# Other rates for the column sums of w_ada and w_in between the weight units

## The chip, the cores and the metric

The kernel runs on one core of a Trainium2 chip. The metric is the time of one execution in microseconds (us) as the device measures it; the lower the better. The core has five engines with queues of their own: TensorE (PE in the profile, its weight loads PEld), VectorE (DVE), ScalarE (ACT), GpSimd (POOL) and SyncE (SP), which issues most of the loads.

## The reference, cut to what matters

One layer of a hybrid decoder, for 512 tokens of width 2048, in float32:

```python
mod = silu(c) @ w_ada + b_ada                       # six rows of 2048
sh_a, sc_a, gt_a, sh_f, sc_f, gt_f = split(mod, 6)
h = rmsnorm(x, norm_mix) * (1 + sc_a) + sh_a
p = h @ w_in                                        # q, k, v, z, c_q, c_kv, k_pe, b, a, gates
y_a = mla(c_q, c_kv, k_pe, ...) @ w_o_mla           # latent attention
y_b = gated_delta_net(q, k, v, z, b, a) @ w_o_gdn   # GDN
g_a, g_b = split(sigmoid(gate_logits), 2)
x = x + gt_a * ((g_a * y_a + g_b * y_b) @ w_o)
h = rmsnorm(x, norm_ffn) * (1 + sc_f) + sh_f
gate, up = split(h @ w_gate_up, 2)
out = rmsnorm(x + gt_f * ((silu(gate) * up) @ w_down), final_norm)
```

`c` is one vector. Each of the six rows of `mod` is therefore 2048 sums of products of one vector with a column of `w_ada`. They are computed on VectorE beside the large products of TensorE, and so is the product of `sh_a` with the columns of `w_in` that belong to the gate `g_a`, which gives that gate a bias.

## The kernel before

**Weight units.** TensorE multiplies in float32r: each operand is split into a rounded part (hi) and the rest (lo), and each product is three matmuls, hi x hi, hi x lo and lo x hi. The work is cut into units. A weight unit loads two 128x512 blocks of a weight (512 KB, SyncE's queue), splits them (ScalarE casts hi at L270, VectorE subtracts lo at L271, both 128x1024) and runs 24 matmuls with 512 columns. kb's units have 12. `Unit` has a `load`, a `split`, and the matmuls `mms`; any of them may be missing.

**The driver** (L51 to L129) takes units from one list. `fill` keeps two units with matmuls ready (`deep`) and four more units of any kind loaded (`ahead`); it calls `load` and `split` in the list's order. `run` emits a unit's matmuls. After each 12 matmuls (`GROUP`) it calls `pump`, which advances each of the side chains by one step: the convolution, the GDN's recursion, the norms of the latents (steps with `cT`, L991 and L250), attention. Those steps have small matmuls of TensorE and operations of VectorE and ScalarE that read their results from PSUM. PSUM has eight banks; a set of weight units holds four of them, and the chains' steps share the rest. The orders on TensorE, SyncE and GpSimd are held as they are written; on VectorE and ScalarE that is so where the code says it, as for the column sums (`late=True`, L443).

**The list** is `mixed(mixing(), extras(), plan)`, L132. `mixing` gives the weight units of the mixer in this order, with the index i that `mixed` counts over all of its units:

- i = 0 loads two small vectors; 1 to 16 the units of the gate logits g_a that the head left over (ga8, ga12)
- 17 to 24 q03, 25 to 32 k03, 33 to 40 v03 (q, k, v of the GDN's heads 0 to 3), 41 to 44 kb (the narrow columns), 45 to 60 gb0 and gb1 (gate logits g_b)
- 61 to 84 q47, k47, v47; 85 to 116 z0, cq, ckv, z1; 117 to 122 qpe, v0, v1; 123 to 130 qk
- 131 to 146 gb2: eight weight units, and ahead of each a unit that only reloads two blocks of the activation h (four tiles of 256 KB) that had been stored to make room; 147 to 154 gb3
- from 155 on ya, yb and w_o; then the channel mixer, whose units do not count (`alone`) or come after the extras are used up

The GDN of heads 0 to 3 runs as a chain from gb0 on, that of heads 4 to 7 from z0 on, attention from qk to the start of ya.

**The extras** (L566) are units without matmuls that `mixed` puts between the weight units. 128 of them are column sums of w_ada, four chunks of 32: a load of 128x1024 (512 KB) and one VectorE operation (`mod_sum`, L442) that multiplies by silu(c) and adds up along the row. The first chunk is the mixer's shift sh_a, without which h isn't complete, then come the channel mixer's scale and shift and the gate gt_a. Number 129 stores gt_a (GpSimd's queue). Numbers 130 to 161 are the column sums of w_in: a load of 512 KB and two VectorE operations (`ada_units`, L384); after each eight of them a chain step brings the sum into columns with four one-column matmuls (`adac`). Behind them the generator gives empty units until attention has ended, then the last chunk of w_ada and the last gate's weights.

**The rate.** `plan(i)` says how many extras follow on the unit with index i. `mixed` adds it up to n and gives one extra for each whole number; a unit marked `alone` adds nothing, but counts in i.

Of the kernel before, what the change touches and what calls it, by code (L numbers as in the profile page):

```python
# [173 lines left out]
def block_kernel(ctx: ExitStack, tc: tile.TileContext, a: dict, out):  # L174
# [17 lines left out]
    def S(s, dt=F32):  # L192
        return slots.tile([P, 512], dt, tag="s", name=nm(s))
# [7 lines left out]
    def load(dst, src):  # L201
        nc.sync.dma_start(dst, src)
# [368 lines left out]
    def head():  # L571
# [39 lines left out]
        for k in range(KT):  # L611
            if k + 1 < KT:
                prepare(k + 1)
            else:
                drv.deep = 1
                drv.open(mixed(everything(), extras(), plan))
            u, head_units[k] = head_units[k], None
            u.pre()
            for m in u.mms:
                m()  # L620
            u.post()
# [617 lines left out]
    def gate_done(n):  # L1239
        def done(ps):  # L1240
            for j in range(4):
                s = S("sg")
                nc.scalar.activation(s[:], ps[j][:], AF.Sigmoid)
                nc.scalar.dma_start(gb_dram[4 * n + j], s[:])
        return done
# [361 lines left out]
    known = set()  # L1607

    def plan(i):
        return 2.0 if i < 16 else 0.7 if i < 48 else 1.0 if i < 150 else 1.2  # L1610

    def act(fn):
        return Unit(load=fn)
# [32 lines left out]
    def reload(k0):  # L1646
        for k in (k0, k0 + 1):
            hN[k] = [S("hh", F32R), S("hl", F32R)]
            for j in range(2):
                load(hN[k][j][:].bitcast(F32), hspill[k, j])  # L1650
# [3 lines left out]
    def w_in_fm(name, c0, done, lo_eng=None):  # L1654
        return fm_set(name, lambda k0, nk: plain(w_in, k0, nk, c0, 512), 512, KT, hx, done, lo_eng=lo_eng)
# [4 lines left out]
    def mixing():  # L1660
# [51 lines left out]
        for n in (2, 3):  # L1712
            us = w_in_fm(f"gb{n}", O_GB + 512 * n, gate_done(n))
            for i, u in enumerate(us):
                if n == 2:
                    yield act(lambda i=i: reload(2 * i))
                yield u
        yv = lambda k: (yT[k][0][:], yT[k][1][:])
        w_om, w_og = a["w_o_mla"][0], a["w_o_gdn"][0]
# [844 lines left out]
    def everything():  # L2564
        yield from mixing()
        yield from ffn()
# [56 lines left out]
```

## Time and profile before

| | |
|---|---|
| median of 3 runs | 2712.14 us (2709.2 to 2715.04) |
| profiled execution, own time | 2706.44 us |
| its span, first to last instruction | 2704.6 us |
| DVE busy | 2087.6 us, 77% of the span |
| ACT busy | 1201.6 us, 44% |
| moved by DMA | 600.45 MB, mean 222 GB/s |
| DVE: sums of w_ada (L442), 192 with the head's 32 and the last chunk's 32 | 233.9 us |
| DVE: sums of w_in (L384), 60 | 44.8 us |
| DVE: lo of the weights (L271), 262 | 320.7 us |

The profile is one execution. Its times run from the first instruction of the program. A row of the busy times by stage has the stretch (from:to), its length, then for each engine the busy time and the number of instructions, the granted clock of TensorE (1.00 is full), the mean busy share of the 16 DMA engines and the rate. A row of waits has who waited, the line of what it waited for and its tile, the sum in us, the number of waits and the longest. A row of a group of instructions has line, engine, operation, what it writes and reads, its shapes, the count, the busy sum in us, the mean of one in ns, and the idle time ahead of it. A row of the timeline has the start, the duration, the instruction, and in brackets the idle time ahead of it with what ended it. All matmuls stand at line 157.

### The profile page before, as it was taken

What the parts mean: (1) busy time and instruction counts of PE and PEld (TensorE: products, weight loads), DVE (VectorE), ACT (ScalarE), POOL (GpSimd) and SP (SyncE); (2) the same over time, 40 slices, a digit from 0 to 9 for tenths busy, and PEclk for the clock granted to TensorE, in tenths of its full rate; (3) what the DMA queues carried; (4) which work ended last, traced back from release to release, by engine and by line L of the source; (5) the groups of instructions that cost most, each with busy time, mean ns of one, the idle gap of its engine ahead of it and who ended that gap; (6) DMA issues with size and microseconds to landing.
All of it is one profiled execution on the core that took longest, in us unless ns stands there. A gap on an engine that the chain in (4) does not pass through costs nothing.

```text
span 2704.6 us, 36528 instructions
## 1 busy us (share of the span) xinstructions
PE 2683.6 (99%) x13046; PEld 2237.3 (83%) x13046; DVE 2087.6 (77%) x3230; ACT 1201.6 (44%) x1720; POOL 228.6 (8%) x310
## 2 busy tenths in 40 slices
PE   9999999999999999999999999999999999999998
PEld 7888788888888888888888888888888888888886
DVE  8785666777768866768788778788878888788786
ACT  3443432453245333234574444444444446545454
POOL 0000002011100000000010000001101101011012
PEclk9999999999999999999999999999999999999999
DMA  9897565646664867854763566567767777788595
GB/s 372 306 351 268 158 192 177 201 152 191 187 172 136 286 223 285 306 187 134 272 193 120 193 209 208 202 218 250 243 227 263 252 249 212 210 238 226 179 278 154
DMA packets 312126, 600.45 MB, mean 222 GB/s; under 512 B 42852, under 2 KB 69636, under 8 KB 311816
## 3 DMA queue, kind: packets, MB, share of 16 engines
q1 hardware_dynamic: 257160, 486.52, 54.7%
q0 software_dynamic: 21888, 59.83, 8.3%
q10 hardware_dynamic: 32896, 51.78, 5.2%
q8 instruction: 102, 1.67, 0.3%
q14 instruction: 80, 0.66, 0.1%
HBM read 507.80 MB, written 90.20 MB: 221 GB/s over the span
## 4 chain that ended last, share of the span: by engine, by line
PE 98%; DVE 1%; ACT 1%; issue 0%; DMA 0%; SPq 0%; DVEq 0%; ACTq 0%
PE m L157 43%; PE gb L157 6%; PE v L157 4%; PE z L157 3%; PE ya L157 3%; PE ga L157 3%; PE k L157 3%; PE s L157 3%; PE q L157 3%; PE yb L157 3%; PE wo L157 3%; PE gu L157 3%; PE dn L157 2%; PE qk L157 2%; PE dnt L157 2%; PE ckv L157 2%
## 5 line engine op out<-in xcount | busy, mean ns | idle before, releaser
L1888 ACT CAST hi<-raws 128x1024 fp32r<-128x1024 f32 (+1 forms) x360 | 322.9, 907 | 575.3 <-DVE raws L1868 346.9
L1895 DVE TENSOR_TENSOR lo<-raws,hi 128x1024 fp32r<-128x1024 f32 (+1 forms) x360 | 376.0, 1046 | 176.5 <-ACT hi L1888 168.9
L270 ACT CAST hi<-raw 128x1024 fp32r<-128x1024 f32 x262 | 271.9, 1041 | 489.8 <-DMA raw<-in_w_in_dram 130.7
L271 DVE TENSOR_TENSOR lo<-raw,hi 128x1024 fp32r<-128x1024 f32 x262 | 320.7, 1227 | 190.2 <-ACT hi L270 183.6
L442 DVE CUSTOM_DVE_ANT_0 rawm<-rawm,cbc 128x1024 f32<-128x1024 f32 x192 | 233.9, 1234 | 3.8 <-DMA rawm<-in_w_mod_dram 3.5
L157 PE MATMUL m<-hi,h2h 128*128 128x512 f32 x480 | 190.7, 397 | 0.0
L157 PE MATMUL m<-hi,h2l 128*128 128x512 f32 x480 | 187.4, 390 | 0.0
L157 PE MATMUL m<-lo,h2h 128*128 128x512 f32 x480 | 186.9, 389 | 0.0
L157 PE MATMUL m<-hi,xh 128*128 128x512 f32 x448 | 174.6, 390 | 0.7 <-DVE al L247 0.7
L157 PE MATMUL m<-hi,xl 128*128 128x512 f32 x448 | 174.4, 389 | 0.0
L157 PE MATMUL m<-lo,xh 128*128 128x512 f32 x448 | 174.4, 389 | 0.0
L1895 DVE TENSOR_TENSOR lo<-sums,hi 128x1024 fp32r<-128x1024 f32 x120 | 146.7, 1222 | 22.2 <-ACT hi L1888 22.1
L1868 DVE TENSOR_TENSOR sums<-raws,raws 128x1024 f32<-128x1024 f32 x120 | 146.2, 1219 | 3.6 <-DMA raws<-in_w_down_dram 3.6
L1888 ACT CAST hi<-sums 128x1024 fp32r<-128x1024 f32 x120 | 126.1, 1051 | 36.1 <-PE m L157 22.5
L157 PEld LDWEIGHTS m<-hi,h2l 128*128 128x128 f32 x480 | 90.1, 188 | 19.4
L157 PEld LDWEIGHTS m<-lo,h2h 128*128 128x128 f32 x480 | 90.4, 188 | 17.8
L157 PEld LDWEIGHTS m<-hi,h2h 128*128 128x128 f32 x480 | 90.2, 188 | 17.3
L157 PE MATMUL gb<-hh,hi 128*128 128x512 f32 x256 | 102.4, 400 | 0.0
L157 PE MATMUL gb<-hh,lo 128*128 128x512 f32 x256 | 100.0, 391 | 0.0
L157 PE MATMUL gb<-hl,hi 128*128 128x512 f32 x256 | 99.9, 390 | 0.0
L157 PEld LDWEIGHTS m<-hi,xh 128*128 128x128 f32 x448 | 84.1, 188 | 18.8 <-DVE al L247 1.1
L157 PEld LDWEIGHTS m<-hi,xl 128*128 128x128 f32 x448 | 84.1, 188 | 17.6
(587 smaller groups left out, 6844.5 us busy)
## 6 DMA issues: line engine op xcount, KB each, us to landing
raws<-in_w_gate_up_dram SPq DMA_DIRECT2D x400, 256.0 KB, 4.0
rawm<-in_w_mod_dram SPq DMA_DIRECT2D x192, 512.0 KB, 5.5
raw<-in_w_in_dram SPq DMA_DIRECT2D x144, 512.0 KB, 5.0
raws<-in_w_down_dram SPq DMA_DIRECT2D x160, 256.0 KB, 5.2
s_dram<-raws ACTq DMA_DIRECT2D x88, 256.0 KB, 3.5
raws<-s_dram SPq DMA_DIRECT2D x88, 256.0 KB, 4.3
rawa<-in_w_in_dram SPq DMA_DIRECT2D x32, 512.0 KB, 5.6
raw<-in_w_o_dram SPq DMA_DIRECT2D x24, 512.0 KB, 6.9
```

Source lines behind the costliest of these rows:

```text
L157: return self.tc.keep_in_program_order(f(*args, **kwargs))
L270: nc.scalar.copy(hi[:], raw[:])
L271: (lo_eng or nc.vector).tensor_tensor(lo[:], raw[:], hi[:].bitcast(F32), ALU.subtract)
L442: r = nc.vector.tensor_tensor_reduce(raw, raw, c, 1.0, 0.0, ALU.mult, ALU.add, parts[:, k, half:half + 1])
L1868: add = lambda o, x, y: behind(nc.vector.tensor_tensor(o, x, y, ALU.add))
L1888: nc.scalar.copy(hi[:], src)
L1895: nc.vector.tensor_tensor(lo[:], src, hi[:].bitcast(F32), ALU.subtract)
```

## The change

Two edits. `plan` gets other rates: 0.6 instead of 0.7 for i from 16 to 25, 1.2 instead of 0.7 or 1.0 from 26 to 59, 0.9 instead of 1.0 from 60 to 115; from 116 on, and below 16, it is as before. And the eight units of gb2 that reload activations are marked `alone`, so that they add nothing to n.

```diff
     def plan(i):
-        return 2.0 if i < 16 else 0.7 if i < 48 else 1.0 if i < 150 else 1.2
+        return 2.0 if i < 16 else 0.6 if i < 26 else 1.2 if i < 60 else 0.9 if i < 116 else 1.0 if i < 150 else 1.2
...
                 if n == 2:
-                    yield act(lambda i=i: reload(2 * i))
+                    yield Unit(load=lambda i=i: reload(2 * i), alone=True)
                 yield u
```

`act(fn)` is `Unit(load=fn)`, so `alone` is the only difference in the second edit.

## The prediction

> **What bounds the kernel now.** I read the page first, then the waits of TensorE, then the busy time by stage of the stretch that the change touches.
>
> ```profile
> span 2704.6 us, 36528 instructions
> PE 2683.6 (99%) x13046; PEld 2237.3 (83%) x13046; DVE 2087.6 (77%) x3230; ACT 1201.6 (44%) x1720; POOL 228.6 (8%) x310
> PEclk9999999999999999999999999999999999999999
> ```
>
> TensorE is busy for 2683.6 of 2704.6 us at the full granted clock; 21.0 us are idle in all. The stages, in the order of the rows below: the two last ga sets, q03, k03 with v03, kb, gb0 with gb1, q47 to v47, z0 to z1, qpe to qk, gb2 with gb3, ya with yb; the last row is the kernel's end.
>
> ```profile
> core 0: us, PE busy (x) PEld busy (x) DVE busy (x) ACT busy (x) POOL busy (x), PEclk, DMA share, GB/s
> 100.00:188.00 88.00, 88.00 (x391) 72.57 (x391) 78.08 (x133) 34.75 (x48) 3.88 (x8) 1.00 0.95 336
> 188.00:232.00 44.00, 44.00 (x195) 36.45 (x195) 30.60 (x40) 18.84 (x25) 2.13 (x4) 1.00 1.00 370
> 232.00:319.00 87.00, 87.00 (x385) 72.07 (x384) 49.13 (x70) 32.62 (x44) 0.00 (x0) 1.00 0.55 171
> 319.00:330.00 11.00, 11.00 (x50) 7.11 (x49) 9.21 (x15) 5.77 (x10) 0.00 (x0) 1.00 0.34 106
> 330.00:431.00 101.00, 101.00 (x500) 84.40 (x498) 65.91 (x125) 34.30 (x44) 16.79 (x11) 1.00 0.60 184
> 431.00:576.00 145.00, 145.00 (x895) 120.93 (x894) 103.39 (x198) 57.72 (x89) 10.79 (x18) 1.00 0.60 188
> 576.00:788.00 212.00, 209.15 (x1244) 175.40 (x1243) 165.58 (x365) 84.49 (x141) 28.85 (x31) 1.00 0.60 181
> 788.00:903.00 115.00, 115.00 (x665) 100.16 (x664) 87.92 (x213) 53.59 (x117) 1.17 (x1) 1.00 0.55 164
> 903.00:1032.00 129.00, 127.72 (x694) 110.09 (x694) 86.90 (x197) 48.30 (x93) 0.00 (x0) 1.00 0.67 229
> 1032.00:1210.00 178.00, 178.00 (x802) 147.36 (x802) 124.71 (x184) 55.19 (x68) 6.60 (x11) 1.00 0.82 285
> 2650.00:2700.00 50.00, 44.26 (x196) 36.32 (x194) 36.30 (x91) 19.64 (x45) 18.42 (x15) 0.99 0.60 149
> ```
>
> Only two of the ten stages have an idle TensorE: 2.85 us in z0 to z1 and 1.28 us in gb2 with gb3, 4.13 us together. That is the whole of what moving sums about between 100 and 1210 us can take out of idle time; the rest lies in the head and the tail, which the change leaves alone. The waits of TensorE between 100 and 1210 us say who ends these idle times, and the rows of one stage ahead say what the weights wait for.
>
> ```profile
> engine line waited for: us in total, times, longest us
> PE cT L157 <- DVE cql L250: 1.6, 1, 1.6
> PE cq L157 <- ACT sz L946: 0.9, 1, 0.9
> PE adac L157 <- DVE yl L247: 0.6, 1, 0.6
> PE sc L157 <- DVE knl L247: 0.5, 1, 0.5
> PE cq L157 <- ACT E L766: 0.3, 1, 0.3
> ...
> ACT hi L270 <- PE gb L157: 47.1, 13, 6.2
> ACT hi L270 <- PE k L157: 23.7, 7, 4.4
> ACT hi L270 <- DMA raw<-in_w_in_dram: 18.0, 8, 6.9
> ```
>
> No wait of TensorE is for a weight (hi or lo of a matmul of this stretch). It is the other way round: in q03 to gb1 the casts of ScalarE (L270) wait for TensorE to give a buffer back. How far ahead they are, DVE's splits and the chain of waits show:
>
> ```profile
> 309.47 1.23 DVE L271 TENSOR_TENSOR lo<-raw,hi 128x1024 fp32r<-128x1024 f32 x1 [4.05 <-ACT hi L270]
> ...
> 319.46 11.04 PE kb L157 x48
> 330.50 8.16 PE gb L157 x36
> ```
>
> This split, counted in the order of the units, is that of gb0's first unit; it ends at 310.70 and its matmuls start at 330.50. The weights are 19.8 us ahead.
>
> **What the change does, counted by hand.** I add up the rate over the unit index i and note each whole number. Numbers 1 to 32 are column sums of w_ada for the mixer's shift, 33 to 128 those of three more chunks, 129 only stores gt_mix, 130 to 161 are the sums of w_in, and after them come empty units until attention ends. Sums that fall in each stage, before and after: ga 32 and 32 (rate 2.0 up to i = 15 is untouched); q03 6 and 5; k03 with v03 11 and 18; kb 3 and 8; gb0 with gb1 15 and 19; q47 to v47 24 and 22; z0 to z1 32 and 29; qpe to qk 14 and 14; gb2 16 and 8; gb3 to i = 154 9 and 9. Nothing is added or removed: 153 and 152 are done when gb2 ends, number 161 falls at i = 153 or 154, and the empty units take up the difference. So from ya on the order is the old one to about a unit. No matmul is added either; each of the four bias sets still makes its few one-column products.
>
> What a sum costs DVE is in these groups:
>
> ```profile
> L442 DVE CUSTOM_DVE_ANT_0 rawm<-rawm,cbc 128x1024 f32<-128x1024 f32 x192 | 233.9, 1234 | 3.8 <-DMA rawm<-in_w_mod_dram 3.5
> L442 DVE DVE_READ_ACCUMULATOR2_ANT parts<- 128x1 f32 x192 | 16.0, 84 | 0.0
> L384 DVE SCALAR_TENSOR_TENSOR acc<-rawa,sh_mix,acc 128x512 f32<-128x512 f32 x60 | 44.8, 747 | 1.2 <-DMA rawa<-in_w_in_dram 0.5
> ```
>
> A w_ada sum is 1.23 + 0.08 = 1.32 us of DVE, a w_in sum two of 0.747, 1.49 us.
>
> *More in the middle.* k03 to kb get 12 more (14 to 26): 15.8 us of DVE. DVE is busy for 49.13 + 9.21 = 58.3 of 98 us there, so it comes to 74 of 98. gb0 with gb1 get 4 more: 65.91 + 5.3 = 71 of 101. Both lie below the 78.08 of 88 that the ga stage carries with TensorE never idle. Were it all laid end to end it would still be less than the 19.8 us by which the weights lead. Each sum loads 128 x 1024 x 4 bytes, 0.52 MB; 12 of them in 98 us add 64 GB/s to the 171 and 106 of these rows, where q03 moved 370. So the cost is 0 by this reckoning. The bounds: not below 0, since no idle time is there to win; above, every added sum could hold up a small chain step, which I price as a rival. I take 0, the nearest row (ga, at rate 2.0 and without idle time) being on that side.
>
> *Fewer behind the head, q47 to z1.* TensorE waits for nothing in q03, so one sum less gains 0. In z0 to z1 the largest wait is cT for cql, and its neighbours on DVE are
>
> ```profile
> 767.37 0.74 DVE L250 SCALAR_TENSOR_TENSOR ckvl<-cT,columns,ckvh 128x512 fp32r<-128x512 f32 x1
> 768.03 1.22 DVE L442 CUSTOM_DVE_ANT_0 rawm<-rawm,cbc 128x1024 f32<-128x1024 f32 x1
> 769.17 0.09 DVE L442 DVE_READ_ACCUMULATOR2_ANT parts<- 128x1 f32 x1
> 769.17 1.22 DVE L442 CUSTOM_DVE_ANT_0 rawm<-rawm,cbc 128x1024 f32<-128x1024 f32 x1
> 770.31 0.09 DVE L442 DVE_READ_ACCUMULATOR2_ANT parts<- 128x1 f32 x1
> 770.31 0.41 DVE L855 TENSOR_SCALAR T64T<-X 32x256 f32<-32x256 f32 x1
> 770.65 0.73 DVE L250 SCALAR_TENSOR_TENSOR cql<-cT,columns,cqh 128x512 fp32r<-128x512 f32 x1
> ...
> 771.44 0.66 PE L157 MATMUL cT<-kc,ckv 128*128 128x128 f32 x4 [1.56 <-DVE cql L250]
> ```
>
> Two sums stand ahead of cql. Counted in their order they are numbers 122 and 123, of z1's last two units. After the change numbers 129 and 130 stand there: a store without DVE work, and a w_in sum. So 2 x 1.22 becomes 1.49 us: 0.9 us less queue, and the wait falls by 0.9 (bounds 0, if cql waits for its matmul or cast instead, and 1.56, all of it). The two waits of cq are for Exp and Silu on ScalarE, with no sum in front: 0. The store itself goes one stage forward; its issue is on GpSimd, busy for 28.85 of 212 us there, and what could come to stand behind it there (the memsets of the GDN's triangular blocks) would wait only for gt_mix, which DVE makes right ahead: 0.
>
> *Reloads not counted.* gb2 gets 8 sums instead of 16: 12 us of DVE and 4.2 MB of loads less. The idle time in this row is the wait of adac for yl (0.6) and of sc for knl (0.5), both on DVE operations that the w_in sums precede. adac also moves by some units, so that its step can meet another step of attention. Bounds: 0 to 1.1 gained; I take 0.4, as adac's wait can come back elsewhere.
>
> **Sum.** -0.9 - 0.4 = -1.3 us. Against the profiled execution (2706.44 us, of which 2704.6 are the span) that is 2705.1; the median of the runs shown is 2712.14, 5.7 above it, and the same -1.3 gives 2710.8.
>
> **A rule that speaks for more.** The steady pace of TensorE in this trace is a matmul each 227 ns:
>
> ```profile
> 232.42 43.52 PE k L157 x192
> L157 PEld LDWEIGHTS m<-hi,h2l 128*128 128x128 f32 x480 | 90.1, 188 | 19.4
> ```
>
> 43.52 / 192 = 0.2267 us, and one weight load takes 0.188, so a stretch without any wait shows 0.188 / 0.2267 = 83% of weight loading. The rows agree: k03 with v03, with no idle time, has 72.07 / 87 = 83%, the same as z0 to z1 (175.40 / 212 = 83%) and the whole span. The Trainium skill, "Trainium Kernel Development and Optimization", section "Performance Expectations", says that busy time of the matmuls is a bad measure of the distance from the limit, and the share of weight loading a good one. By that rule 17% of the span could be open, and a better order of the sums could win more than the 4.13 us. By these rows it isn't: 83% is what an uninterrupted stream gives here.
>
> **Rivals.** (1) *All idle time of the stretch goes.* For it: three of the five waits are on DVE. Against: the two of cq are not. It gives 2712.14 - 4.1 = 2708.0. (2) *Hidden slack of the pipeline*: matmuls that the page counts as busy start late behind small steps, and less DVE work shortens that. It would have to be over 1.3 us on top of (1), 2706.7 or less. Against it: the equal 83% above. (3) *Slower: DVE's queue in gb0 and gb1.* There the GDN's first half begins, one step for 12 matmuls (2.7 us), and each step's PSUM read is on DVE. If the added sums stand in front of these reads as the two did in front of cql, each such place costs up to 1.56 us. It decides from the point where DVE runs more than a step, 2.7 us, behind; four places make 6.2 us, 2718.4. For it: 19 sums instead of 15, and DVE at 71 of 101 us. Against: 32 sums in z0 to z1, with DVE at 165.58 of 212, made one such place. (4) *No effect*: the empty units absorb the count, cql is held by the new sum as long as by the old ones, and the median stays at 2712.1.
>
> **How the numbers follow.** My forecast has a chance of 0.70, (1) 0.12, (2) 0.03, (3) 0.07, (4) 0.08. A measurement can tell about 0.2%, 5.4 us. Only (2) passes it on the fast side, and (1) where scatter of the runs adds 1.3 us, half of its chance: with a little for what I overlook, 0.11. On the slow side (3) and a little: 0.09. The rest, 0.80, is the same. The range: the lowest run shown is the profiled one, 2706.44; less both DVE terms at their ends (1.56 + 1.1) that is 2703.8. The highest is 2715.04, and one new place of 1.56 us makes 2716.6.
>
> **What would show it.** Right: cT's wait for cql under 1 us; the cq waits as they are; DVE at about 74 us in k03 to kb and about 12 us less in gb2, where the DMA rate falls too; TensorE without a wait between 188 and 576 us. Wrong: new waits of TensorE for DVE in gb0 and gb1, or for a hi or lo; a wait of over 2 us anywhere in the stretch; or a matmul pace in k03 other than 227 ns.

## The result and the profile after

| | before | after |
|---|---|---|
| median of 22 runs each, side by side | 2711.26 us | 2713.51 us |
| ratio, 95% interval | | 1.0013 [1.0007, 1.0019] |
| profiled execution | 2706.44 us | 2713.24 us |
| its span | 2704.6 us | 2711.4 us |

The change makes the kernel slower by 0.13%, 3.5 us (1.9 to 5.2). The ratio goes by the fast runs alone, without one of before at 2982.46 us, and so isn't the quotient of the two medians, which lie 2.3 us apart. The loss is less than the 0.2% named in the prediction and inside its range, but the interval does not contain 1, and the forecast pointed the other way: -1.3 us. The two profiled executions lie 6.8 us apart; the one of before is among the fastest of its kernel.

The page's lines on the span and the engines, after:

```profile
span 2711.4 us, 36526 instructions
PE 2687.3 (99%) x13046; PEld 2240.2 (83%) x13046; DVE 2084.2 (77%) x3230; ACT 1200.9 (44%) x1720; POOL 234.3 (9%) x310
```

TensorE does the same 13046 matmuls. Its waits between 100 and 1210 us, after, in the columns of the prediction's view:

```profile
PE X L157 <- issue: 3.9, 5, 1.1
PE gb L157 <- DVE yl L247: 1.2, 2, 0.6
PE cq L157 <- ACT sz L946: 0.9, 1, 0.9
PE sc L157 <- DVE knl L247: 0.5, 1, 0.5
PE cq L157 <- ACT E L766: 0.3, 1, 0.3
```

The wait of cT for cql is gone, as forecast. The largest is new: 3.9 us in X, the 32x32 products of the GDN's second half, for which the profile shows no releaser ("issue"). By stage, after, k03 with v03, kb, gb0 with gb1, and z0 to z1 (columns as in the prediction):

```profile
232.00:319.00 87.00, 87.00 (x386) 72.06 (x385) 56.49 (x87) 30.34 (x42) 0.00 (x0) 1.00 0.64 208
319.00:330.00 11.00, 11.00 (x49) 7.17 (x48) 9.39 (x14) 7.10 (x12) 0.00 (x0) 1.00 0.37 108
330.00:431.00 101.00, 101.00 (x497) 84.28 (x496) 70.78 (x137) 35.01 (x45) 16.81 (x11) 1.00 0.69 214
576.00:788.00 212.00, 206.76 (x1199) 172.84 (x1198) 156.04 (x349) 81.80 (x139) 30.01 (x32) 0.98 0.55 163
```

Of these rows only z0 to z1 (576 to 788) lost anything: TensorE is idle for 5.24 us instead of 2.85, and the granted clock is 0.98. (gb2 with gb3, 903 to 1032, went from 1.28 us of idle time to 1.69.) The order of events there, on TensorE, first before (start, duration, instruction):

```profile
769.10 0.19 PE L157 MATMUL X<-T32T,M 32*32 32x32 f32 x1
...
771.44 0.66 PE L157 MATMUL cT<-kc,ckv 128*128 128x128 f32 x4 [1.56 <-DVE cql L250]
771.85 0.48 PE L157 MATMUL z<-hi,hh 128*128 128x512 f32 x1
...
773.99 0.39 PE L157 MATMUL z<-hi,hh 128*128 128x512 f32 x1
```

and after:

```profile
769.18 0.19 PE L157 MATMUL X<-M,T32T 32*32 32x32 f32 x1
770.13 0.22 PE L157 MATMUL X<-T32T,M 32*32 32x32 f32 x2 [0.76 <-issue]
...
774.47 0.21 PE L157 MATMUL X<-T32T,M 32*32 32x32 f32 x1 [0.96 <-issue]
...
774.80 0.24 PE L157 MATMUL X<-T32T,M 32*32 32x32 f32 x1
...
775.87 1.06 PE L157 MATMUL cT<-kc,ckv 128*128 128x128 f32 x4
776.58 0.78 PE L157 MATMUL z<-hi,hh 128*128 128x512 f32 x1
...
780.53 0.39 PE L157 MATMUL z<-hi,hh 128*128 128x512 f32 x1
```

Read the starts. The last X is 5.70 us later than before (774.80 against 769.10); the first z only 4.73 (776.58 against 771.85), since cT no longer waits 1.56, though its own matmuls are slower (1.11 and 1.06 us instead of 0.66); its tenth matmul 6.54 (780.53 against 773.99), because nine z matmuls take 3.95 us instead of 2.14, some 427 ns apart: TensorE runs at half clock. The granted clock reads 0.50 from 773.6 to 780.5 us, so it fell already between the last stops. From there the difference moves between 6.1 and 8.3 us, as waits of about 1 us come and go in attention and gb2, and ends at 6.9: +0.4 by these, and 0.45 had been there from the head on.

What stands beside it is the store of gt_mix. GpSimd's row of it, before:

```profile
804.89 1.17 POOL L157 DMA_DIRECT2D m_dram<-gt_mix  x1 [40.05 <-DVE gt_mix L449]
```

and after:

```profile
763.36 1.17 POOL L157 DMA_DIRECT2D m_dram<-gt_mix  x1 [19.43 <-DVE gt_mix L449]
```

It writes 128x16 values of 4 bytes, each to an address of its own: 2048 pieces, 8 KB. (The pieces are counted from the address pattern in the code; the DMA view lists this store as 48 packets.) The DMA view of 763 to 776 us has the rate in 40 slices of 0.325 us, and each issue's size and median time to landing. Before:

```profile
GB/s 202 252 254 254 378 266 235 96 203 271 252 290 240 169 109 113 214 214 302 328 265 101 44 154 206 310 317 304 213 151 210 184 301 328 302 202 50 0 0 0
raw<-in_w_ukv_dram SPq DMA_DIRECT2D x4, 256.0 KB, 4.0
```

and after:

```profile
GB/s 326 304 265 186 180 230 323 284 257 174 93 29 8 0 0 0 0 0 0 0 0 2 6 17 46 19 6 5 6 25 14 5 11 3 14 14 27 27 71 217
raw<-in_w_ukv_dram SPq DMA_DIRECT2D x2, 256.0 KB, 10.6
```

From 766.9 us on hardly anything moves for 8 us, and two weight blocks that are asked for at its start, at 767.2 and 767.6 us, take 10.6 us in the median instead of 4.0. The X burst (64 products, 128 matmuls and 128 weight loads) falls into this gap. The trace of before had shown the price of the store in its own place; the same view there, 803 to 822 us, slices of 0.475 us:

```profile
GB/s 0 86 121 345 405 192 129 216 255 274 204 49 1 0 0 0 4 39 69 52 34 60 22 39 22 22 39 26 22 134 328 392 267 136 142 309 318 217 46 22
m_dram<-gt_mix POOLq DMA_DIRECT2D x1, 8.0 KB, 10.5
```

8 KB take 10.5 us to land, and the rate falls to between 0 and 70 GB/s for about 8 us, in a stretch (788 to 903 us) in which TensorE never waits.

### The profile page after: what moved, and what is told of

Its sections match the earlier page's. It is cut to its first block, busy times and chain, and to the rows that moved or that the text cites. A ratio compares the mean times of both kernels' runs of the same rounds, so it can differ in the third digit from the quotient of the medians.

```text
span 2711.4 us, 36526 instructions
## 1 busy us (share of the span) xinstructions
PE 2687.3 (99%) x13046; PEld 2240.2 (83%) x13046; DVE 2084.2 (77%) x3230; ACT 1200.9 (44%) x1720; POOL 234.3 (9%) x310
## 4 chain that ended last, share of the span: by engine, by line
PE 98%; DVE 1%; ACT 1%; DMA 0%; issue 0%; SPq 0%; DVEq 0%; ACTq 0%
PE m L157 43%; PE gb L157 6%; PE v L157 4%; PE z L157 3%; PE ya L157 3%; PE k L157 3%; PE ga L157 3%; PE q L157 3%; PE s L157 3%; PE yb L157 3%; PE wo L157 3%; PE gu L157 3%; PE dn L157 2%; PE dnt L157 2%; PE ckv L157 2%; PE cq L157 2%
```

## The experiments

Theory A: the store's 2048 small pieces hold up the other DMA traffic, and a dense burst on TensorE that meets this gap stops, and the clock falls with it. Its rival B: the sums moved on DVE are the cost, and X only stands where it shows.

**One edit alone, and the store itself.** Four kernels beside the kernel before (33 runs, median 2709.57 us). The first has the new rates only (its edit against the changed kernel):

```diff
-                    yield Unit(load=lambda i=i: reload(2 * i), alone=True)
+                    yield act(lambda i=i: reload(2 * i))
```

> Only the new rates; the reloads of gb2 count as before. Theory A (the store of gt_mix into m_dram in 4-byte pieces keeps the DMA engines from moving anything else for about 10 us; the new rates put it at 763 us, right ahead of the GDN's burst of 32x32 matmuls at 768, whose instructions then don't arrive): number 129 stays at z1's last but one unit, so the waits of the X matmuls for issue (3.9 us) and the slow matmuls behind them are there, and the time is that of the changed kernel, 1.0010 to 1.0015 of before. Rival B (the sums that no longer follow the reloads in gb2 are what costs): as before, 0.9995 to 1.0005. Rival C (the added sums in k03 to gb1 hold up VectorE): as A in time, but with waits of TensorE for DVE between 232 and 441 us.

2713.2 us, 1.0013 [1.0004, 1.0022]: all of the loss, with the store at 763.18 us and TensorE's wait

```profile
PE X L157 <- issue: 4.1, 4, 2.2
```

The second has `alone` only (the old `plan`):

> Only the second edit, with the old rates. Theory A: number 129 falls at v1 as before, its store is issued near 805 us, the X matmuls at 768 run without a wait: within 0.05% of before, or up to 1 us faster by the waits of gb2. Rival B: slower by the 3 us of the changed kernel, 1.0013. Rival C: as before.

2711.93 us, 1.0007 [0.9999, 1.0016]; the store stays late, at 807.56 us, and X does not wait. The time is not told apart from before. The profiled execution isn't free of waits, though: cT waits for ckvl (2.2 us, two times) and cql (1.6), and gb once for yl, behind which half clock follows, as TensorE's rows show:

```profile
909.57 0.65 PE L157 MATMUL gb<-hh,hi 128*128 128x512 f32 x1 [2.42 <-DVE yl L247]
910.02 0.63 PE L157 MATMUL gb<-hl,hi 128*128 128x512 f32 x1
910.44 0.63 PE L157 MATMUL gb<-hh,lo 128*128 128x512 f32 x1
```

The third is the changed kernel with the store moved behind the sums of w_in, and an empty unit in its place:

```diff
-        yield Unit(split=lambda: side(m_dram.rearrange("(k p) -> p k", p=P), gt_mix[:]))
-        known.add(4)
+        yield Unit()
...
+        yield Unit(split=lambda: side(m_dram.rearrange("(k p) -> p k", p=P), gt_mix[:]))
+        known.add(4)
```

> The changed kernel with an empty unit in place of number 129, and the store of gt_mix behind the four sums of w_in (number 162, in ya). Theory A: no wait for issue at 770 us, the matmuls behind the burst run at 227 ns; 5 to 6 us less than the changed kernel, 2707 to 2709, which is also below before by 2 to 4 us. Rivals B and C: the loss stays, 1.0010 to 1.0015 of before.

2707.14 us, 0.9992 [0.9983, 1.0000], no wait in X. The store did not go where I meant it to: GpSimd had nothing else to do, so it was issued only a few instructions later, behind the memsets of TT, which wait for TensorE. Its row, and TensorE's stretch (columns as in the prediction's rows by stage):

```profile
770.52 1.18 POOL L157 DMA_DIRECT2D m_dram<-gt_mix  x1 [0.30 <-issue]
```

```profile
770.00:775.00 5.00, 5.00 (x150) 4.39 (x150) 2.78 (x6) 2.53 (x6) 1.40 (x2) 1.00 0.53 107
775.00:780.00 5.00, 5.00 (x28) 4.18 (x27) 3.85 (x6) 4.87 (x11) 0.00 (x0) 1.00 0.00 0
```

Seven microseconds are enough: the burst (the row with 150 matmuls) is through before the gap, and then 5 us without any traffic cost TensorE nothing. (Part of that silence is that nothing was asked for: SyncE issued no load between 769.7 and 777.7 us.) The fourth leaves the store in place and writes rows of 64 bytes, 128 pieces instead of 2048. The gate then comes back in another order, so this kernel serves for its time alone:

```diff
-        yield Unit(split=lambda: side(m_dram.rearrange("(k p) -> p k", p=P), gt_mix[:]))
+        yield Unit(split=lambda: side(m_dram.rearrange("(p k) -> p k", p=P), gt_mix[:]))
```

> The changed kernel with the same store at the same place, but written in 64-byte rows instead of 4-byte pieces (the gate gt_mix of w_o comes back permuted, so the output is another). Theory A, if the pieces are the cause: as e3, 5 to 6 us below the changed kernel, with the DMA rate from 766 to 776 us near 200 GB/s instead of under 20. If any store at that place does it: the loss stays. Rivals B and C: the loss stays.

2707.07 us, 0.9989 [0.9980, 0.9998], no wait in X. The same queue and 8 KB, issued at 763.52, land in 3.5 us instead of 10.5, and the two weight blocks asked for at 767.4 and 767.9 us in 3.2 instead of 10.6 (DMA view, 763 to 776 us):

```profile
raw<-in_w_ukv_dram SPq DMA_DIRECT2D x2, 256.0 KB, 3.2
m_dram<-gt_mix POOLq DMA_DIRECT2D x1, 8.0 KB, 3.5
```

So it is neither the queue nor the bytes, but into how many pieces they are cut.

**The suspect added to the kernel before.** A copy of 128x16 values, stored in the same 4-byte pieces to a tensor that nobody reads, with the place of the sums unchanged (beside the kernel before: 30 runs, 2709.65 us, for these four):

```diff
+            if n == 24:
+                def again(split=u.split):
+                    split()
+                    behind(nc.vector.tensor_copy(twin[:], parts[:, :, 0]))
+                    side(d_dram.rearrange("(k p) -> p k", p=P), twin[:])
+                u.split = again
...
```

> The kernel before, with a second store in 4-byte pieces: behind sum number 121 a copy of a 128x16 tile goes to a tensor that nobody reads, so that it is issued near 764 us, where the changed kernel has its store. Nothing else of the order changes. Theory A (a store in 4-byte pieces just ahead of the 32x32 burst takes the instructions of TensorE away): waits of the X matmuls for issue of 3 to 5 us and slow matmuls behind them; 4 to 6 us slower than before, 1.0015 to 1.0022. Rival D (the rates do it in another way and the store is only a sign): as before, 0.9997 to 1.0003.

2716.07 us, 1.0023 [1.0013, 1.0033]. The second store, at 763.12 us, brings the whole picture into the kernel before:

```profile
PE X L157 <- issue: 3.6, 3, 1.7
PE cT L157 <- DVE cql L250: 1.6, 1, 1.6
```

with 62 and 20 GB/s between 765 and 775 us. No sum was moved, and the loss is there: rival B isn't needed for it. The counterpart, the kernel before with its only store later (the third kernel's edit):

> The kernel before with an empty unit as number 129 and the store behind the w_in sums (number 162, in ya), as in the run of the changed kernel with a late store. It tells what the rates are worth without the store: if the step of the prediction on cql and adac is right, this is 1 to 2 us slower than the changed kernel with the late store (2707.1). Theory A: the place at 805 us costs the kernel before something in part of its runs (its runs spread from 2706.6 to 2715.3), so 1 to 2 us below before. If the place at 805 us is free: as before.

2709.59 us, 1.0000 [0.9991, 1.0009]. It tells little: the store left at 805.15 us, where it had been. GpSimd has nothing else to issue between the two places in the list, so in both kernels the store goes as soon as gt_mix is there.

**The other half of the condition.** The changed kernel with the store as it is, and the X burst of the second half three steps sooner:

```diff
-        yield 6
+        yield 3 if g else 6
...
-        yield
+        yield 4 if g else 1
```

> The changed kernel, where the second GDN half's burst of 32x32 matmuls (X) comes three steps, 8 us, sooner, near 760 us, and the next step waits three steps longer, so the rest stays. The store in 4-byte pieces stays near 764 to 768 us. Theory A with the burst as the second condition: no wait of X for issue, 4 to 6 us below the changed kernel, though the DMA rate has its gap of 8 to 10 us as there. If the store alone costs the time (weights or loads late): the loss stays at 1.0010 to 1.0015 of before.

2706.40 us, 0.9987 [0.9978, 0.9995], the lowest median here; its interval overlaps those of the third and the fourth kernel. The store takes as long as ever, and the rate shows the same gap, though in part because SyncE asks for nothing between 763.5 and 771.5 us here (DMA view, 763 to 776 us):

```profile
GB/s 148 279 254 199 82 195 208 321 328 177 147 74 46 3 2 0 0 0 0 0 0 0 0 0 0 0 0 0 0 0 0 0 0 0 0 8 14 65 173 340
m_dram<-gt_mix POOLq DMA_DIRECT2D x1, 8.0 KB, 10.5
```

but the burst ran at 758 us, and TensorE has matmuls of 512 and 128 columns in it:

```profile
765.00:770.00 5.00, 5.00 (x31) 4.27 (x30) 1.54 (x3) 4.89 (x11) 0.41 (x1) 1.00 0.40 83
770.00:775.00 5.00, 5.00 (x27) 4.16 (x26) 4.01 (x6) 3.58 (x6) 0.00 (x0) 1.00 0.07 1
```

The loss needs both, store and burst, at one time; either alone costs nothing that these runs show. Next, the changed kernel with the store in four parts of 512 pieces, each behind the eight sums that it belongs to:

```diff
+        def gate_done4(ks):
+            mod_columns(gt_mix, ks, b_cols[:, GT_A // P:GT_A // P + 16])
+            side(m_dram.rearrange("(k p) -> p k", p=P)[:, ks], gt_mix[:, ks])
...
+        yield Unit()
```

> The changed kernel with the store of gt_mix in four parts of 512 pieces, each issued when its four columns are ready (sums 104, 112, 120 and 128), and an empty unit as number 129. Theory A: each part takes a quarter of the 10 us, 2 to 3 us of a low DMA rate; the last, at 763 us, is over when the burst needs its instructions, so no wait for issue or under 1 us of it; 4 to 6 us below the changed kernel, 2707 to 2709. If the number of pieces doesn't set the length: loss as in the changed kernel.

2711.3 us, 1.0007 [0.9998, 1.0016]: a miss. The last quarter, at 765.26 us, still stops X:

```profile
PE X L157 <- issue: 1.3, 2, 1.1
```

A quarter of the pieces leaves a third of the wait, and the time is not told apart from that of before. The control for the sooner burst is the same edit in the kernel before (15 runs, 2710.52 us):

> The kernel before with its own rates, and only the burst of 32x32 matmuls (X) of the GDN's second half three steps sooner, the wait behind it three steps longer, as in the fastest kernel so far. Theory A (the store beside the burst is what costs; the place of the burst by itself is worth nothing): in the kernel before the store lies 40 us behind the burst, so nothing is there to win: the time of the kernel before within 1 us, ratio 0.9996 to 1.0004, no wait in X in either place, and the 2.5 to 3 us that the kernel with the changed rates and the sooner burst is faster than before belong to the rates. Rival (the sooner burst is itself what is worth those 2.5 to 3 us, because small steps of the GDN come free sooner): 2706 to 2707, ratio 0.9987 to 0.9992, and the idle time of TensorE between 760 and 790 us falls.

2709.8 us, 0.9999 [0.9990, 1.0008]. X does not wait in it. The burst's place by itself is worth nothing that can be measured; where the store doesn't disturb it, there is nothing to win.

**What X waits for.** TensorE's instructions seem to be loaded in blocks: one instruction queue shows 102 packets of 16 KB, and 13046 matmuls with as many weight loads make about 256 instructions for each. In the profiles the first stop fell near a block's end. So two kernels put more instructions ahead of the burst, by doing small products of an earlier step twice or more, which moves the blocks' ends within the burst (the first of them; cut to the lines that matter):

```diff
+                    for _ in range(2 if g and c < 3 else 1):
+                        mm(p1[pb:pb + 32, n0:n0 + 32], LT[c][pa:pa + 32, 128 * i + pb:128 * i + pb + 32],
+                           T32[pa:pa + 32, n0:n0 + 32], start=True, stop=True, tile_position=(pa, pb))
```

and the other with `2 + c % 2 if g else 1`.

> The changed kernel with 24 of the 32 small products into M1 (the step six steps ahead of the X burst, second half of the GDN) done twice with the same operands: 24 products of two matmuls and two weight loads each are 96 more instructions of TensorE's stream ahead of the burst, about 0.4 us of work; store and burst stay where they were. In the four profiles with the wait, X first stops about 183 to 193 records behind the start of the burst, and that is 252 to 273 records behind the fetch of a block of TensorE's instructions before it (blocks of 256). Theory A1 (it is the instruction stream that runs dry beside the store: the stop stands at a block's end): the first stop comes about 96 records sooner, 85 to 100 records behind the start of the burst; the wait is 3 to 5 us in all, the time 2712 to 2716 us. Rival A2 (something that each instruction writes or takes runs full, a count from the burst's start): the first stop stays at 183 to 193 records of the burst.

> The changed kernel with the 32 small products into M1 done two or three times: 48 products more, 192 instructions of TensorE's stream ahead of the burst, about 0.8 us of work; store and burst stay where they were. Theory A1 (instruction stream): the end of the block falls within 10 records of the start of the burst and the next one at its end, so the burst either stops near its start (up to record 10) or, if the fetch of the next block has time enough, not at all or only at its last records. Rival A2 (a count from the burst's start): the first stop stays at 183 to 193 records of the burst with the same 4 us.

1.0008 [0.9997, 1.0019] and 1.0012 [1.0001, 1.0024], with 2.1 and 4.4 us of waits in X. TensorE's rows with a stop in X, with 96 more:

```profile
771.95 0.50 PE L157 MATMUL X<-T32T,M 32*32 32x32 f32 x2 [1.82 <-issue]
773.58 0.50 PE L157 MATMUL X<-T32T,M 32*32 32x32 f32 x2 [0.26 <-issue]
```

and with 192 more:

```profile
771.43 0.18 PE L157 MATMUL X<-T32T,M 32*32 32x32 f32 x1 [1.33 <-issue]
774.70 0.25 PE L157 MATMUL X<-T32T,M 32*32 32x32 f32 x1 [3.08 <-issue]
```

Counted in the trace, matmuls and weight loads, the first stop stands 197 and 189 instructions behind the start of the burst; in the four earlier profiles with the wait it was 183 to 193. It did not move by 96 or 192: the end of a block is not what stops X. The five stops in the changed kernel agree, for they lie within 25 instructions, and a block's end could make one of them. The Trainium skill, "Runtime: NRT & Kernel Launch", section "Instruction fetch mechanics", says that crossing such a block costs little and is mostly hidden; in these two runs no stop goes with a block's end. What remains is a count: some 190 instructions of the burst pass within 1.0 to 1.2 us, and then TensorE stops. That something fills up which only the DMA's traffic can empty would fit, but no run here shows it. Nor is it settled where the count starts: from the issue of the store to the first stop it is 230 to 246 matmuls and weight loads, about as constant. Every run here, the timed ones too, comes with its span and granted clock, so all seem to have been recorded; whether an execution without a record would stop as well is not known.

## Why the prediction was wrong

**The step that failed** is the one on the store: "The store itself goes one stage forward; its issue is on GpSimd [...] what could come to stand behind it there [...]: 0." It asked what stands behind the store on its issuing engine, and not what stands behind it in the DMA engines. Its price was 3.9 us of stops and 1.8 us by half clock in the nine z matmuls behind them, in the profiled execution. The runs: adding such a store costs 1.0023; taking it out of the burst's way, by later issue, larger pieces or a sooner burst, gives 0.9992, 0.9989, 0.9987. The place could have been seen, too: the units were counted far enough to put number 129 into z1's last units, where X runs, and the landing time of 10.5 us for 8 KB stood in the trace of before.

**Two sums ahead of cql, -0.9.** Right, and more than forecast: the wait vanished, 1.56, the bound that was named. It isn't the stop of X that gave DVE the time, for the wait is gone too in the kernels without a stop (late store, 64-byte rows, sooner burst). The forecast left a w_in sum of 1.49 us ahead of cql; with 64-byte rows DVE shows no sum at all between 763 and 775 us. In the changed kernel the gain was given back in the same 10 us.

**gb2, -0.4.** Not seen; it came out as +0.4, outside the bounds of 0 to 1.1 gained. adac's wait for yl went, but gb now waits for yl (1.2 us, two times): a step of attention meets a DVE queue at another unit, as feared. The sizes were off as well: in 903 to 967 us DVE is busy for 44.64 us instead of 49.42, 4.8 less and not 12, as the next rows show (before, then after):

```profile
903.00:967.00 64.00, 63.34 (x358) 55.05 (x358) 49.42 (x122) 23.30 (x50) 0.00 (x0) 1.00 0.81 285
```

```profile
903.00:967.00 64.00, 62.93 (x353) 54.60 (x352) 44.64 (x112) 23.16 (x50) 0.00 (x0) 1.00 0.78 264
```

**More sums in the middle, 0.** Right: no wait of TensorE between 188 and 576 us. In k03 to kb DVE came to 56.49 + 9.39 = 65.9 us, not 74. Part of that is a slip in the count: kb has four units, which at a rate of 1.2 give 5 sums and not 8, so that 9 more were due, 11.9 us. The trace has 8 more (22 instead of 14 operations on rawm between 232 and 330 us) and DVE 7.5 us more. In gb0 with gb1 it came to 70.78, the forecast's 71. The cost of 0 doesn't hang on the slip.

**The rivals.** (3), DVE's queue in gb0 and gb1, did not occur; the slow side came by a mechanism that none of them named. (4) is refuted by cql's wait. (1) did not occur as described: both waits of cq are still there. (2) was not tested. Without the meeting of store and burst the changed kernel runs at 0.9987 to 0.9992 of before, 2.2 to 3.5 us less; the forecast ratio for -1.3 us, 0.9995, lies at the edge of these intervals or within them, so the sum of its terms may have been right in size, or somewhat small; by time alone (1)'s -4.1 us would fit as well. Where more than cql's 1.6 us came from was not settled, but one pattern points to it: in all five profiles with the old rates cT waits for cql or ckvl, 1.6 to 3.8 us in all (3.8 with `alone` only, 2.0 with the sooner burst), and in none of the eight with the new ones. The trace from which the prediction took 1.56 us is that of one of the shortest executions (2706.44 us), and so may have shown the least of it.

## What to carry to other kernels

When a step is moved, move its transfer in your mind as well: look up in the DMA view how long it takes to land and what the rate is beside it, and then ask which dense stretch of small instructions it will meet. Here a store of 2048 4-byte pieces, only 8 KB, was a traffic jam of about 8 us; put such a store where TensorE runs large matmuls, or give it longer rows. And a small edit's gain (1.6 us here) is worth less than one such meeting (about 6 us).

## What the hardware showed that I had not expected

- 2048 pieces of 4 bytes, 8 KB, took 10.1 to 11.6 us to land where the profile has the landing, with the other traffic at 0 to 70 GB/s for about 8; in 128 pieces of 64 bytes 3.5 us.
- Larger matmuls (512 and 128 columns) passed through the gap without a stop (5.00 of 5.00 us at 1 GB/s); the burst of small ones stopped after some 190 instructions. It may be the number and not the size: with the sooner burst only 114 matmuls and weight loads fall between the issue and the landing of the store.
- Half clock, 427 ns between matmuls, came after five stops of 3.9 us in all (the granted clock 0.50 for 6.8 us) and after a single wait of 2.42 us (for 3.4 us), but not after the 1.56 us before cT, nor after the three waits of 1.09, 1.15 and 1.56 us between 764 and 775 us with `alone` only. In the kernel with the added store it came even behind a wait of 1.28 us:

```profile
912.87 0.51 PE L157 MATMUL gb<-hh,hi 128*128 128x512 f32 x1 [1.28 <-DVE yl L247]
...
913.85 0.63 PE L157 MATMUL gb<-hh,hi 128*128 128x512 f32 x1
914.28 0.63 PE L157 MATMUL gb<-hl,hi 128*128 128x512 f32 x1
```

  The Trainium skill, "TensorE: Matmul & The Clock Gate", section "Part 1: The HAM clock gate (the "warmup" mystery)", has the clock halved after an idle window of about 3.4 us that runs freely, and full again after as long a busy one. The return agrees: half clock lasted 3.4 or 6.8 us, one or two such windows. The condition does not, if an idle window is one without any matmul: waits of 1.28 and 2.42 us were enough, and 1.56 us was not, so the length of one wait didn't decide it here.
